# Feed-forward entries of a two-layer hybrid decoder: the clear of the last covered tile is put ahead of the step's remainder, and its values stay in that step; in the first pass the values go one step later

## The chip, the cores and the metric

The kernel runs on one core of a Trainium2 chip. Times are device microseconds (us) of one execution of the whole program. TensorE (PE) multiplies, VectorE (DVE) and ScalarE (ACT) work elementwise, GpSimd (POOL) and SyncE (SP) start most of the DMA transfers. Each engine works through its own list of instructions in order and waits on semaphores for the others.

## The reference

Two layers; each has a half-step feed-forward block, three token mixers side by side, and a second half-step feed-forward block. The change is in the feed-forward blocks alone, of which there are four in the program ("passes" below).

```python
def swiglu(h, w_in, w_out):
    gate, up = jnp.split(h @ w_in, 2, axis=-1)
    return (jax.nn.silu(gate) * up) @ w_out

for l in range(DEPTH):                                   # DEPTH = 2
    x = x + 0.5 * swiglu(rms_norm(x, ffn1_norm[l]), ffn1_w_in[l], ffn1_w_out[l])
    h = rms_norm(x, mix_norm[l]) @ w_mix_in[l]
    ...
    x = x + y @ w_mix_out[l]
    x = x + 0.5 * swiglu(rms_norm(x, ffn2_norm[l]), ffn2_w_in[l], ffn2_w_out[l])
```

x is 512 tokens by 1024 channels in float32, the hidden width is 2816.

## The kernel before, in words

Everything lies transposed: channels or hidden units on the 128 partitions, the 512 tokens along the free axis. A float32 product is made from three passes of the array: both operands are split into a rounded high part and the rest (`hi`, `lo`), and `mm3` (lines 318 to 333) issues high times high, high times low, low times high. A weight tile of 128 x 1024 is split by ACT, which copies the high part (line 801, `hl<-w`), and by DVE, which subtracts it (line 803).

The hidden units of a feed-forward block are done in two ways. The first `covered` tiles of 128 units (six in the first pass, four in the others) are plain products with the not yet normalised x, one pair of tiles at a time, while the norm and the operands of the second way are still being made. The rest goes through a Strassen-like scheme of seven products per pair of tiles, P1 to P7, each of 24 matmuls of 256 columns. These products are the *steps* of the block, numbered from 0. `halved` (line 757) runs them; in step n it issues product n, then `prepare` for the product three steps later (`LEAD = 3`: ACT's copy at once, DVE's subtraction kept as `rest`), then the elementwise work on the product's result, then whatever `self.between` holds for n, then `rest`, then the planned sums of weights (`run(n)`, line 789 among them), and last whatever `self.entry` holds for n. The order of seven products is P1, P2, P6, P5, P7, P3, P4. In the passes after the first, steps 0 to 6 and 7 to 13 are two such blocks, and step 18 is the first product of the output side, which has `m` as moving operand (line 755 makes its low part).

The results of a covered tile stay in two PSUM banks until they are *cleared*: DVE multiplies both by the reciprocal norm (`gi`, line 562, and `ui`, line 563), ACT puts `gi` through SiLU (line 274). Then the *values*: DVE multiplies `gi` by `ui` in two halves (lines 701 and 704) into the quarter tiles `hq` of the hidden activations. In passes 2 to 4 the last covered tile is cleared by the entry of step 13 and its values are the entry of step 14:

```python
        self.entry = {
            ...
            13: lambda: clear(2, 1),
            14: lambda: values(2, 1),
        }
        self.between = {4: lambda: lows["P4"]()}
```

In the first pass the loop over `halved` does both for a tile behind step 1 and for the other tile behind step 3 (lines 468 to 471). Other lines that the prediction speaks of: 904 and 888 (ACT copies the negated P1 and P6 results out of PSUM), 907 (DVE, behind P2), 916 and 919 (ACT behind P5, DVE adds the bank after P7), 922 (DVE, behind P3). P1, P6, P7 and P4 add up in one bank, so P6 can start only when line 904 has read it and P4 only when line 919 has.

Of the kernel before, what the change touches and what calls it, by code (L numbers as in the profile page):

```python
# [157 lines left out]
class Trunk:  # L158
# [292 lines left out]
    def ffn(self, w_in, w_out, next_gain, covered, begin=None, out=None):  # L451
        nc = self.nc
        tc = self.tc
        with tc.tile_pool(name=self.n("ffn"), bufs=1) as fp:
            self.tt, self.tb = "g2", 2
            if begin is not None:
                x, gain, logits = begin
            self.hq = {}
            self.entry = {}
            self.final = out is not None  # L460
            halved = self.halved(fp, w_in, w_out, covered)
            if begin is None:
                self.enter(fp, w_in, halved)
                for _ in halved:
                    pass
            else:
                finish = self.cover(fp, w_in, covered, begin, halved)
                for n, _ in enumerate(halved):

                    if n in (1, 3):  # L470
                        finish(n // 2)

            f0, nf = CHUNKS[-1]
            if next_gain is not None:
                self.begin_norm(next_gain)
            self.ntog += 1
            if out is not None:
                self.way_out(w_out, out, f0, nf)
                return
            for dg in range(2):  # L480
                banks = self.next4()

                def parts(k, kk, dg=dg):
                    r = slice((f0 + k) * P, (f0 + k + kk) * P)
                    return [w_out[r, dg * 512 : (dg + 1) * 512]]

                self.stream(
                    [(bk, slice(c, c + P), None) for bk, c in zip(banks, (0, 128, 256, 384))],
                    parts, self.last_hidden, nf,
                )  # L490
                for i in range(4):
                    j = dg * 4 + i
                    xj = self.xT[:, j, :]
                    nc.vector.scalar_tensor_tensor(
                        out=xj, in0=banks[i], scalar=0.5, in1=xj,
                        op0=ALU.mult, op1=ALU.add,
                    )
                    if next_gain is not None:
                        self.norm_part(j, fp)

    def cover(self, fp, w_in, covered, begin, then):
        nc = self.nc
        x, gain, logits = begin
        for f in range(0, covered, 2):
            banks = self.next4()

            def parts(k, kk, f=f):
                r = slice(k * P, (k + kk) * P)
                return [w_in[r, f * P : (f + 2) * P], w_in[r, FF + f * P : FF + (f + 2) * P]]

            opening = f == 0

            def norm():
                self.end_norm(
                    self.bank("pt" if self.ntog % 2 == 0 else "po"), fp,
                    self.parted_norm(fp, ("r0", "r1"), 1),
                )
                self.xparts = self.halves_of_x(fp)

                for _ in range(2):  # L520
                    next(self.xparts)


            jobs = [(bk, slice(c, c + P)) for bk, c in zip(banks, (0, 256, 128, 384))]
            if opening:
                nt = iter(["xh4", "xl4", "xh5", "xl5", "xh6", "xl6", "r2", "r3", "r4", "r5"])
                consts = self.build_consts(
                    lambda dt: fp.tile([P, T], dt, tag=next(nt), name=self.n("c"))
                )
                self.open_stream(x, gain, fp, parts, jobs, consts)  # L530
            else:
                self.stream([(*j, None) for j in jobs], parts, self.xact, KD, queued=f == 2)
            if opening:
                for _ in consts:
                    pass
                norm()
                self.lower_bounds(logits, fp.tile([P, T], F32, tag="g1", name=self.n("lb"), bufs=2))
            if f == 2:
                for _ in self.xparts:
                    pass  # L540
            if f + 4 == covered or f + 2 == covered:
                next(then)
            if opening:
                self.table(SILU)

            def finish(i, f=f, banks=banks):
                self.finish(fp, f, i, banks[2 * i], banks[2 * i + 1], f + 2 == covered)

            if f + 2 < covered:
                for i in range(2):  # L550
                    finish(i)
        return finish

    def finish(self, fp, f, i, pg, pu, keep):
        self.values(fp, f, i, *self.clear(fp, pg, pu, keep), keep)

    def clear(self, fp, pg, pu, keep):
        nc = self.nc
# [14 lines left out]
    def enter(self, fp, w_in, then):  # L573
# [68 lines left out]
        cleared = {}  # L642

        def clear(f, i):
            banks = bb if f else ba
            cleared[f, i] = self.clear(fp, banks[2 * i], banks[2 * i + 1], True)

        def values(f, i):
            self.values(fp, f, i, *cleared.pop((f, i)), True)
# [34 lines left out]
            7: lambda: values(0, 1),  # L684
            9: lambda: clear(2, 0),
            10: lambda: values(2, 0),
            13: lambda: clear(2, 1),
            14: lambda: values(2, 1),
        }
        self.between = {4: lambda: lows["P4"]()}  # L690

    def quarter(self, fp, c, a, b):
        if (c, a, b) not in self.hq:
# [327 lines left out]
    def mix(self, l, w, w_out, conv_w, out_gain, q_gain, k_gain, f_bias, next_gain):  # L1021
# [3 lines left out]
        with tc.tile_pool(name=self.n("mix"), bufs=1) as mp:  # L1025
# [181 lines left out]
            def most():  # L1207
                for dg in range(4):
# [5 lines left out]
                    for i in range(2):  # L1214
                        add(2 * dg + i, banks[i])

            beside(attend, conv(), 1, finish)
            beside(self.fox_attend(ap1, 1, half[1], qkg, {}), most())
            self.ntog = 0
# [651 lines left out]
```

## Time and profile before

| | |
|---|---|
| median of three runs | 1811.73 us (1809.85 to 1812.07) |
| the profiled execution | 1810.12 us, of which its span (first to last instruction) 1808.3 us |
| granted TensorE clock | 1.000 |
| PE busy | 1796.7 us, 99% of the span |
| DVE busy | 1453.1 us, 80% |
| ACT busy | 1000.3 us, 55% |
| POOL busy | 170.3 us, 9% |
| all DMA queues | 250.94 MB, mean 139 GB/s |

How to read it: a busy share is an average over the program, and in a profile with PE busy nearly throughout, what counts is where PE's matmuls are spaced wider than usual. The timeline lists instructions by start and duration in us; what stands in brackets at a row's end is how long the engine idled just before and what ended that. Matmuls overlap in the pipeline (each row is longer than the distance to the next one), so lost time is read from the distances between starts.

### The profile page before, as it was taken

What the parts mean: (1) busy time and instruction counts of PE and PEld (TensorE: products, weight loads), DVE (VectorE), ACT (ScalarE), POOL (GpSimd) and SP (SyncE); (2) the same over time, 40 slices, a digit from 0 to 9 for tenths busy, and PEclk for the clock granted to TensorE, in tenths of its full rate; (3) what the DMA queues carried; (4) which work ended last, traced back from release to release, by engine and by line L of the source; (5) the groups of instructions that cost most, each with busy time, mean ns of one, the idle gap of its engine ahead of it and who ended that gap; (6) DMA issues with size and microseconds to landing.
All of it is one profiled execution on the core that took longest, in us unless ns stands there. A gap on an engine that the chain in (4) does not pass through costs nothing.

```text
span 1808.3 us, 34748 instructions
## 1 busy us (share of the span) xinstructions
PE 1796.7 (99%) x14267; PEld 1681.8 (93%) x14267; DVE 1453.1 (80%) x2036; ACT 1000.3 (55%) x1437; POOL 170.3 (9%) x172
## 2 busy tenths in 40 slices
PE   9999999999999999999999999999999999999999
PEld 7899999899888899999889999998998888999997
DVE  8889787776887898879678887876868878888893
ACT  5455554464786465556445555555547855555551
POOL 0011120100000001112001111201000000020210
PEclk9999999999999999999999999999999999999999
DMA  7668783233323757868265687813333246687762
GB/s 204 181 141 187 177 180 99 71 80 83 88 77 111 218 135 164 196 161 167 82 206 132 161 190 195 167 65 83 77 90 88 72 142 184 164 156 194 157 136 94
DMA packets 243486, 250.94 MB, mean 139 GB/s; under 512 B 18520, under 2 KB 228192, under 8 KB 243328
## 3 DMA queue, kind: packets, MB, share of 16 engines
q1 hardware_dynamic: 189424, 182.38, 33.6%
q0 software_dynamic: 53600, 66.09, 23.1%
q8 instruction: 112, 1.84, 0.4%
q14 instruction: 46, 0.38, 0.1%
q10 hardware_dynamic: 304, 0.27, 0.0%
HBM read 223.98 MB, written 2.10 MB: 125 GB/s over the span
## 4 chain that ended last, share of the span: by engine, by line
PE 91%; DVE 4%; ACT 3%; issue 1%; DMA 1%; SPq 0%; ACTq 0%; DVEq 0%
PE mm L322 13%; PE mm L330 13%; PE mm L331 13%; PE sc L330 6%; PE sc L331 6%; PE sc L322 6%; PE pt L322 6%; PE pt L330 6%; PE pt L331 6%; PE po L322 4%; PE po L330 4%; PE po L331 4%; PE po L1607 1%; ACT hl L311 1%; PE pt L1649 1%
## 5 line engine op out<-in xcount | busy, mean ns | idle before, releaser
L801 ACT CAST hl<-w 128x1024 fp32r<-128x1024 f32 x322 | 336.7, 1049 | 308.7 <-PE mm L331 81.9
L803 DVE TENSOR_TENSOR hl<-w,hl 128x1024 fp32r<-128x1024 f32 x322 | 392.1, 1221 | 82.6 <-ACT hl L801 82.6
L312 DVE TENSOR_TENSOR hl<-st,hl 128x512 fp32r<-128x512 f32 (+3 forms) x192 | 162.1, 844 | 106.1 <-ACT hl L311 105.3
L311 ACT CAST hl<-st 128x512 fp32r<-128x512 f32 (+3 forms) x192 | 142.6, 743 | 170.4 <-PE po L331 64.6
L322 PE MATMUL mm<-xc,hl 128*128 128x256 f32 (+1 forms) x733 | 201.6, 276 | 0.2 <-DVE u L919 0.2
L330 PE MATMUL mm<-xc,hl 128*128 128x256 f32 x728 | 201.4, 277 | 0.0
L331 PE MATMUL mm<-xc,hl 128*128 128x256 f32 x728 | 201.1, 276 | 0.0
L322 PE MATMUL sc<-xc,hl 128*128 128x256 f32 (+1 forms) x532 | 146.0, 276 | 0.0
L330 PE MATMUL sc<-xc,hl 128*128 128x256 f32 x528 | 146.0, 276 | 0.0
L331 PE MATMUL sc<-xc,hl 128*128 128x256 f32 x528 | 145.8, 276 | 0.0
L322 PEld LDWEIGHTS mm<-xc,hl 128*128 128x128 f32 x733 | 137.4, 188 | 0.6 <-DVE u L919 0.4
L330 PEld LDWEIGHTS mm<-xc,hl 128*128 128x128 f32 x728 | 136.8, 188 | 0.0
L331 PEld LDWEIGHTS mm<-xc,hl 128*128 128x128 f32 x728 | 136.7, 188 | 0.0
L322 PE MATMUL pt<-xc,hl 128*128 128x256 f32 (+1 forms) x482 | 132.8, 276 | 0.0
L330 PE MATMUL pt<-xc,hl 128*128 128x256 f32 x480 | 132.6, 276 | 0.0
L331 PE MATMUL pt<-xc,hl 128*128 128x256 f32 x480 | 132.5, 276 | 0.0
L322 PE MATMUL mm<-x,hl 128*128 128x512 f32 x272 | 107.4, 395 | 0.0
L331 PE MATMUL mm<-x,hl 128*128 128x512 f32 x272 | 106.5, 391 | 0.0
L330 PE MATMUL mm<-x,hl 128*128 128x512 f32 x272 | 106.2, 390 | 0.0
L322 PEld LDWEIGHTS sc<-xc,hl 128*128 128x128 f32 x532 | 99.7, 188 | 0.2
L331 PEld LDWEIGHTS sc<-xc,hl 128*128 128x128 f32 x528 | 99.1, 188 | 0.0
L330 PEld LDWEIGHTS sc<-xc,hl 128*128 128x128 f32 x528 | 99.1, 188 | 0.0
(513 smaller groups left out, 5591.4 us busy)
## 6 DMA issues: line engine op xcount, KB each, us to landing
w<-in_ffn_w_in_dram SPq DMA_DIRECT2D x140, 512.0 KB
w<-in_ffn_w_out_dram SPq DMA_DIRECT2D x64, 512.0 KB
w<-in_ffn_w_out_dram POOLq DMA_DIRECT2D x56, 512.0 KB, 8.7
st<-in_w_mix_in_dram SPq DMA_DIRECT2D x88, 256.0 KB
st<-in_ffn_w_in_dram SPq DMA_DIRECT2D x70, 256.0 KB
w<-in_ffn_w_in_dram POOLq DMA_DIRECT2D x35, 512.0 KB, 8.0
w<-S POOLq DMA_DIRECT2D x35, 512.0 KB, 4.7
st<-in_ffn_w_out_dram SPq DMA_DIRECT2D x24, 512.0 KB
```

Source lines behind the costliest of these rows:

```text
L311: a = nc.scalar.copy(hi, src[:, c : c + w])
L312: b = nc.vector.tensor_sub(lo, src[:, c : c + w], hi)
L322: i = nc.tensor.matmul(acc[:, c], ah, bh[:, c], start=first and c.start == 0, stop=False, skip_group_check=True,)
L330: nc.tensor.matmul(acc, a, b, start=False, stop=False, skip_group_check=True)
L331: i = nc.tensor.matmul(acc, c, d, start=False, stop=last, skip_group_check=True)
L801: A(nc.scalar.copy(hi, src))
L803: return lambda: V(nc.vector.tensor_sub(lo, src, hi))
L1607: nc.tensor.matmul(self.ob[:, t0 + u * P : t0 + 2 * P], V[:, j, h % 4].rearrange("p a d -> p (a d)"), part[:, j, u:, :].rearrange("p i t - ...
L1649: nc.tensor.transpose(tb[:, j * P : (j + 1) * P], p[:, j * P : (j + 1) * P], self.ident)
```

## The change

In passes 2 to 4 `clear(2, 1)` moves from the entry of step 13 to `between` of step 13, that is ahead of the step's remaining subtraction, and `values(2, 1)` from the entry of step 14 to that of step 13. In the first pass the values of the second tile move from behind step 3 to behind step 4, while its clear stays. The method `finish`, which did both in one, is gone.

```diff
             else:
-                finish = self.cover(fp, w_in, covered, begin, halved)
+                clear, values = self.cover(fp, w_in, covered, begin, halved)
                 for n, _ in enumerate(halved):
-
                     if n in (1, 3):
-                        finish(n // 2)
+                        cleared = clear(n // 2)
+                    if n in (1, 4):
+                        values(n // 3, cleared)
...
-            13: lambda: clear(2, 1),
-            14: lambda: values(2, 1),
+            13: lambda: values(2, 1),
         }
-        self.between = {4: lambda: lows["P4"]()}
+        self.between = {4: lambda: lows["P4"](), 13: lambda: clear(2, 1)}
```

The lists of PE, ACT, POOL and SP keep their order; only DVE's changes, in four places. The first is in the first pass, steps 3 and 4: DVE before the change, from the clear on (`gi`, `ui`), with line 919 as `u`, line 922 as `g`, and the planned sum `S`:

```order
L562 TENSOR_TENSOR gi_925<-pt_652,inv_401 128x512
L563 TENSOR_TENSOR ui_926<-pt_653,inv_401 128x512
L701 SCALAR_TENSOR_TENSOR hq_860<-gi_925,ui_926 128x256
L704 TENSOR_TENSOR hq_862<-gi_925,ui_926 128x256
L919 TENSOR_TENSOR u_145_920<-u_145_920,mm_788 128x512
L803 TENSOR_TENSOR hl_956<-w_820,hl_956 128x1024
L789 TENSOR_TENSOR S_960<-w_782,w_820 128x1024
L922 TENSOR_TENSOR g_141_888<-g_141_888,mm_893 128x512
```

The same place with the change (its line numbers are two or three higher from here on):

```order
L565 TENSOR_TENSOR gi_925<-pt_652,inv_401 128x512
L566 TENSOR_TENSOR ui_926<-pt_653,inv_401 128x512
L921 TENSOR_TENSOR u_145_920<-u_145_920,mm_788 128x512
L805 TENSOR_TENSOR hl_954<-w_820,hl_954 128x1024
L791 TENSOR_TENSOR S_958<-w_782,w_820 128x1024
L703 SCALAR_TENSOR_TENSOR hq_860<-gi_925,ui_926 128x256
L706 TENSOR_TENSOR hq_862<-gi_925,ui_926 128x256
L924 TENSOR_TENSOR g_141_888<-g_141_888,mm_893 128x512
```

The two halves of the values have moved behind the read of the bank, the subtraction and the sum.

The second place is the end of step 13 and step 14 in the second pass; the third and fourth pass read alike but for their numbers. DVE before, from the last instruction on product 13 to the low part of `m`:

```order
L701 SCALAR_TENSOR_TENSOR hq_7397<-g_1063_7427,pt_7400 128x512
L803 TENSOR_TENSOR hl_7622<-S_7564,hl_7622 128x1024
L562 TENSOR_TENSOR gi_7629<-mm_6930,inv_6946 128x512
L563 TENSOR_TENSOR ui_7630<-po_6931,inv_6946 128x512
L803 TENSOR_TENSOR hl_7659<-w_7303,hl_7659 128x1024
L789 TENSOR_TENSOR w_7431<-S_7564,w_7532 128x1024
L704 TENSOR_TENSOR hq_7159<-gi_7629,ui_7630 128x256
L701 SCALAR_TENSOR_TENSOR hq_7161<-gi_7629,ui_7630 128x256
L907 TENSOR_TENSOR g_1086_7661<-g_1086_7661,pt_7669 128x512
L803 TENSOR_TENSOR hl_7694<-w_7566,hl_7694 128x1024
L755 TENSOR_TENSOR m_7700<-hq_7397,m_7699 128x1024
```

And with the change:

```order
L703 SCALAR_TENSOR_TENSOR hq_7397<-g_1063_7427,pt_7400 128x512
L565 TENSOR_TENSOR gi_7626<-mm_6930,inv_6946 128x512
L566 TENSOR_TENSOR ui_7627<-po_6931,inv_6946 128x512
L805 TENSOR_TENSOR hl_7622<-S_7564,hl_7622 128x1024
L706 TENSOR_TENSOR hq_7159<-gi_7626,ui_7627 128x256
L703 SCALAR_TENSOR_TENSOR hq_7161<-gi_7626,ui_7627 128x256
L805 TENSOR_TENSOR hl_7661<-w_7303,hl_7661 128x1024
L791 TENSOR_TENSOR w_7431<-S_7564,w_7532 128x1024
L909 TENSOR_TENSOR g_1086_7663<-g_1086_7663,pt_7669 128x512
L805 TENSOR_TENSOR hl_7694<-w_7566,hl_7694 128x1024
L757 TENSOR_TENSOR m_7700<-hq_7397,m_7699 128x1024
```

`gi` and `ui` stand ahead of the subtraction from `S`, the two halves of the values ahead of the next subtraction and sum; from `g` (line 907 before) on the order is as it was.

More of the change, by code (lines that the diff above doesn't have):

```diff
@@ L544, in cover, with clear, values @@
                 self.table(SILU)
-            def finish(i, f=f, banks=banks):
-                self.finish(fp, f, i, banks[2 * i], banks[2 * i + 1], f + 2 == covered)
-            if f + 2 < covered:
+            keep = f + 2 == covered
+            def clear(i, banks=banks, keep=keep):
+                return self.clear(fp, banks[2 * i], banks[2 * i + 1], keep)
+            def values(i, cleared, f=f, keep=keep):
+                self.values(fp, f, i, *cleared, keep)
+            if not keep:
                 for i in range(2):
[L551 to L555, printed above, removed]
+                    values(i, clear(i))
+        return clear, values
     def clear(self, fp, pg, pu, keep):
```

## The prediction

> **What bounds the kernel now.** First the page's busy times, then the list of waits for PE, then PE's timeline around the four places where the change moves something, and last DVE's and ACT's timelines there.
>
> ```profile
> PE 1796.7 (99%) x14267; PEld 1681.8 (93%) x14267; DVE 1453.1 (80%) x2036; ACT 1000.3 (55%) x1437; POOL 170.3 (9%) x172
> ```
>
> PE is busy for all but about 12 us of the 1808.3 us span, so the only time to be won lies in places where a matmul starts late. The list of PE's waits (engine and line <- what it waited for: us in total, times, longest) has three entries beside the moved instructions:
>
> ```profile
> PE mm L330 <- DVE m L755: 0.4, 2, 0.2
> ...
> PE mm L322 <- DVE u L919: 0.2, 1, 0.2
> PE sc L330 <- DVE m L755: 0.2, 1, 0.2
> ```
>
> That makes one wait for line 919 (first pass) and three for the low part of `m` (one for each later pass). Matmuls overlap, so these idle times understate the loss; it is read from the starts. PE's timeline in the first pass, end of step 5 and beginning of step 6 (start, duration):
>
> ```profile
> 91.95 0.28 PE L330 MATMUL mm<-xc,hl 128*128 128x256 f32 x1
> ...
> 92.40 0.28 PE L331 MATMUL mm<-xc,hl 128*128 128x256 f32 x1
> 92.88 0.38 PE L322 MATMUL mm<-xc,hl 128*128 128x256 f32 x1 [0.20 <-DVE u L919]
> 93.10 0.28 PE L330 MATMUL mm<-xc,hl 128*128 128x256 f32 x1
> ```
>
> Four regular distances (91.95 to 92.40, three rows left out in between) take 0.45 us, so one is 0.113. From 92.40 to 93.10 are two, which should take 0.225 and take 0.70: the wait costs 0.475 us, the slow distance behind it included. PE's timeline in the second pass, at the start of step 16 (P6) and of step 18 (the first product with `m`):
>
> ```profile
> 669.27 0.28 PE L331 MATMUL pt<-xc,hl 128*128 128x256 f32 x1
> 669.44 0.38 PE L322 MATMUL pt<-xc,hl 128*128 128x256 f32 x1
> 669.66 0.29 PE L330 MATMUL pt<-xc,hl 128*128 128x256 f32 x1
> 669.79 0.28 PE L331 MATMUL pt<-xc,hl 128*128 128x256 f32 x1
> ...
> 675.00 0.28 PE L322 MATMUL mm<-m,hl 128*128 128x256 f32 x1
> 675.48 0.38 PE L330 MATMUL mm<-m,hl 128*128 128x256 f32 x1 [0.20 <-DVE m L755]
> 675.70 0.28 PE L331 MATMUL mm<-m,hl 128*128 128x256 f32 x1
> ```
>
> Step 18 loses 0.70 - 0.225 = 0.475 us. Step 16 loses time too, though too little to be listed as a wait: three distances take 0.52 in place of 0.34, so 0.18. The same spot in passes 3 and 4:
>
> ```profile
> 994.52 0.28 PE L331 MATMUL po<-xc,hl 128*128 128x256 f32 x1
> 994.70 0.38 PE L322 MATMUL mm<-xc,hl 128*128 128x256 f32 x1
> 994.92 0.29 PE L330 MATMUL mm<-xc,hl 128*128 128x256 f32 x1
> ...
> 1562.96 0.28 PE L331 MATMUL pt<-xc,hl 128*128 128x256 f32 x1
> 1563.13 0.38 PE L322 MATMUL pt<-xc,hl 128*128 128x256 f32 x1
> 1563.36 0.29 PE L330 MATMUL pt<-xc,hl 128*128 128x256 f32 x1
> ```
>
> Two distances take 0.40 for 0.225: 0.175 lost in each. Their `m` waits have the same 0.2 in the list as the second pass, so I take the same 0.475.
>
> **The change part by part.** It adds and removes no instruction and no transfer; it moves instructions of DVE past others of DVE.
>
> *First pass.* DVE's timeline there, from the second multiplication of the clear on:
>
> ```profile
> 90.62 0.68 DVE L563 TENSOR_TENSOR ui<-pt,inv 128x512 f32<-128x512 f32 x1
> 91.47 0.43 DVE L701 SCALAR_TENSOR_TENSOR hq<-gi,ui 128x256 f32<-128x256 f32 x1 [0.17 <-ACT gi L274]
> ...
> 92.15 0.68 DVE L919 TENSOR_TENSOR u<-u,mm 128x512 f32<-128x512 f32 x1
> 92.74 1.22 DVE L803 TENSOR_TENSOR hl<-w,hl 128x1024 fp32r<-128x1024 f32 x1
> 93.88 1.22 DVE L789 TENSOR_TENSOR S<-w,w 128x1024 f32<-128x1024 f32 x1
> 95.02 0.68 DVE L922 TENSOR_TENSOR g<-g,mm 128x512 f32<-128x512 f32 x1
> ```
>
> Line 919 reads the bank that step 6 (P4) is waiting for. Its own product, P7, ended a whole product (24 x 0.113 = 2.7 us) before 92.4, so it could have run at 90; it stood behind two halves of values, which also waited 0.17 for SiLU. Rows without a wait follow each other after 0.60 (512 columns), 0.34 (256) and 1.14 (1024). With the values out of the way line 919 starts at 90.62 + 0.60 = 91.22 in place of 92.15 and frees the bank at about 91.95, ahead of the 92.51 at which P4 is due. The wait goes: -0.475 us. What is late next: the values now run behind the sum, and line 922 comes behind them. At worst (sum no earlier than before) it starts at 95.02 + 0.67 = 95.69, 0.67 late; at best the 0.93 gained ahead is kept and it starts 0.26 early. Behind it stands the subtraction for product 8, which starts by 96.29 and is usable 1.28 later (as from the start of the low part of `m`, 674.20 in a row below, to its matmul at 675.48), at 97.6; product 8 starts at 92.51 + 2 x 2.71 = 97.9 and wants the low part with its third matmul at 98.2. A margin of 0.6 remains, so this costs nothing; POOL's next accumulating transfer, which waits for this subtraction, starts up to 0.7 us later, and no weight transfer stands in PE's list. Bounds for the part: -0.475 and, should the margin fail by all of the 0.67, +0.2; I take -0.475.
>
> *Passes 2 to 4.* DVE's timeline in the second pass as it was:
>
> ```profile
> 665.47 1.22 DVE L803 TENSOR_TENSOR hl<-S,hl 128x1024 fp32r<-128x1024 f32 x1
> 666.61 0.68 DVE L562 TENSOR_TENSOR gi<-mm,inv 128x512 f32<-128x512 f32 x1
> 667.21 0.68 DVE L563 TENSOR_TENSOR ui<-po,inv 128x512 f32<-128x512 f32 x1
> 668.93 1.23 DVE L803 TENSOR_TENSOR hl<-w,hl 128x1024 fp32r<-128x1024 f32 x1 [1.04 <-ACT hl L801]
> ...
> 671.88 0.68 DVE L907 TENSOR_TENSOR g<-g,pt 128x512 f32<-128x512 f32 x1
> 672.47 1.22 DVE L803 TENSOR_TENSOR hl<-w,hl 128x1024 fp32r<-128x1024 f32 x1
> 674.20 1.23 DVE L755 TENSOR_TENSOR m<-hq,m 128x1024 fp32r<-128x1024 f32 x1 [0.51 <-ACT m L755]
> ```
>
> and ACT's:
>
> ```profile
> 667.32 0.63 ACT L274 ACTIVATE gi<-gi 128x512 f32<-128x512 f32 x1 [2.08 <-DVE gi L562]
> 667.86 1.03 ACT L801 CAST hl<-w 128x1024 fp32r<-128x1024 f32 x1
> 668.80 0.59 ACT L904 ACTIVATE g<-pt 128x512 f32<-128x512 f32 x1
> ...
> 672.59 0.63 ACT L274 ACTIVATE g<-g 128x512 f32<-128x512 f32 x1 [1.91 <-DVE g L907]
> 673.13 1.04 ACT L755 CAST m<-hq 128x1024 fp32r<-128x1024 f32 x1
> ```
>
> The two engines hand one chain to and fro: clear on DVE, SiLU, copy and line 904 on ACT (PE's step 16 waits for 904), and DVE stands still for 1.04 us until the copy is done. Then sum, values, 907, again SiLU, and only behind it ACT's copy of `m`, DVE's low part, step 18.
>
> With the change: `gi` 665.47, `ui` 666.07, subtraction from `S` 666.67, values 667.81 and 668.15. SiLU follows its `gi` by 0.71 as it does now, at 666.18, and ends around 666.8, a microsecond ahead of the values. ACT's copy behind it also waits for the end of product 14 (24 distances before 669.38, so 666.67); I give the signal half a microsecond and let it start at 667.17 in place of 667.86. Line 904 follows by 0.94 at 668.11 and ends by 668.7, ahead of the 669.38 at which P6 is due. So 0.18 (0.175 in passes 3, 4) goes. DVE's next subtraction starts at 668.48 (its copy, started 1.07 ahead in the rows, is ready at 668.24: no standstill), the sum at 669.62, line 907 at 670.76 in place of 671.88. SiLU 671.47, copy of `m` 0.54 later at 672.01, low part 1.07 behind that (674.20 - 673.13) at 673.08, done at 674.36. Step 18 now starts at 675.00 - 0.18 and wants it with the second matmul at 674.95: a margin of 0.59. The `m` wait goes too, -0.475. What is late next is the subtraction from `S`, 1.2 us later and ready at 667.95; product 16 wants it with its third matmul at 669.61, a margin of 1.66. No transfer waits for that one; those that wait for the others start earlier.
>
> All this leans on the distances of 0.60 and 1.14, each 0.08 shorter than the row's own duration. The Trainium skill, in "VectorE: DVE Perf Modes", section "The DRAIN you can't avoid", says that the next Vector operation doesn't start until the pipe is empty, while adding that one that isn't held starts earlier. Taken strictly, that would put the seven instructions from `gi` to 907 0.08 later each, 0.56 in all, and the margin of 0.59 would be gone; the rows here start before their predecessor's end, so the trace sides with the exception.
>
> Sum: 0.475 + (0.18 + 0.475) + 2 x (0.175 + 0.475) = 2.43 us. Against the profiled execution (1810.12, which is the span plus 1.8) that gives 1807.7; the median of the three runs lies 1.6 above the profiled one, and from it the time is 1811.73 - 2.4 = 1809.3.
>
> **The rivals.**
>
> *Only the small waits go* (chance 0.13). The `m` wait stays in passes 2 to 4, because line 907 or the copy of `m` comes less early than worked out; it takes 0.59 us of error in a chain of eight instructions. For it speaks that the chain changes engine four times; against it that every hop is taken from a row. Gain 0.475 + 0.18 + 2 x 0.175 = 1.0: 1810.7.
>
> *The gain doesn't reach the end* (0.07): PE arrives 2.4 us earlier in all, and the mixers' chains through DVE and ACT, which cause PE's longest waits, take it back: 1811.7. Against it: these chains start from PE's products and would move along.
>
> *More than the sum* (0.14): the runs shown and the profiled one lie in two pairs, at 1810 and at 1812. Where the median of the changed kernel falls into the lower pair, the sum gives 1809.85 - 2.4 = 1807.4, 4.3 below the median of before.
>
> *Slower* (0.06): the clear, now in front of the subtraction from `S`, doesn't find its inputs or buffers free and holds DVE. There are two buffers each of `gi` and `ui`, shared with the blocks' own `g` and `u`. If it had to wait for the end of product 15 (669.4, say 669.6 with the signal), the subtraction would be ready at 669.6 + 1.2 + 1.28 = 672.1, 2.5 us behind P6's 669.61; with the slow distance 2.6, three times 7.8, less the first pass's gain: 1811.7 + 7.3 = 1819.0. It decides from a wait of 1.66 us on. Against it: the buffers' last readers are DVE's own instructions just ahead, and the banks have been full since long before step 13.
>
> **How the numbers follow.** The forecast has the remaining 0.60: 1809.3. About 0.2% of this time, 3.6 us, is what a measurement of this kernel can tell from no change. The three runs spread by 2.2, so a forecast of -2.4 passes -3.6 in about one case in six of its 0.60, 0.10; with the case of more than the sum that makes 0.24 faster. Slower is its rival's 0.06; 0.70 remain within 0.2%. The range leaves out the slower rival and the tails: from 1807.0 (just under the lower pair less 2.4) to 1811.9 (no gain).
>
> **What would show it.** In the changed kernel's PE list the entries for line 919 and line 755 are gone; the distances at the starts of steps 16 and 18 are 0.11; DVE's 1.04 standstill ahead of its subtraction in step 14 is gone, and line 907 there starts 1.4 us behind the end of product 15 (670.76 against 669.38) where it was 2.5. A row naming `hl` with `S` as PE's releaser at step 16, or DVE waiting for SiLU at the values, would make it wrong.

## The result and the profile after

| | before | changed |
|---|---|---|
| median | 1811.4 us (21 runs, 1809.85 to 1812.47) | 1808.03 us (21 runs, 1806.67 to 1810.77) |
| ratio | | 0.9983, 95% interval 0.9977 to 0.9989 |
| span of the profiled execution | 1808.3 us | 1806.7 us |

The changed kernel is faster by 0.17%, 2.0 to 4.2 us by the interval; the sum on record, 2.43 us, is a ratio of 0.9987 and lies inside. The time came in at 1808.0 where 1809.3 was forecast. The forecast that the change stays within 0.2% (3.6 us) held narrowly: the medians differ by 3.4 us.

PE's list of waits of the changed kernel, whole (engine and line <- what it waited for: us in total, times, longest; all line numbers here but 322 are two higher than before):

```profile
PE pt L1651 <- DVE T L1473: 2.6, 2, 1.5
PE mm L1765 <- DVE z L1752: 1.2, 1, 1.2
PE po L1609 <- ACT PH L1653: 0.8, 2, 0.4
PE sc L1586 <- DVE nm L1591: 0.7, 2, 0.4
PE pt L1651 <- DVE KB L1571: 0.4, 2, 0.2
PE mm L322 <- DVE zf L1125: 0.4, 1, 0.4
PE sc L1586 <- DVE fo L1623: 0.2, 1, 0.2
PE po L1609 <- DVE PL L1654: 0.2, 1, 0.2
```

The line that read the bank (919, now 921) and the one that makes the low part of `m` (755, now 757) are gone from it. PE's timeline at the three kinds of place, first step 6 of the first pass, then steps 16 and 18 of the second:

```profile
92.72 0.28 PE L331 MATMUL mm<-xc,hl 128*128 128x256 f32 x1
92.83 0.28 PE L322 MATMUL mm<-xc,hl 128*128 128x256 f32 x1
...
669.47 0.28 PE L331 MATMUL pt<-xc,hl 128*128 128x256 f32 x1
669.59 0.28 PE L322 MATMUL pt<-xc,hl 128*128 128x256 f32 x1
669.70 0.28 PE L330 MATMUL pt<-xc,hl 128*128 128x256 f32 x1
...
675.03 0.28 PE L322 MATMUL mm<-m,hl 128*128 128x256 f32 x1
675.14 0.28 PE L330 MATMUL mm<-m,hl 128*128 128x256 f32 x1
```

Each distance is 0.11 now, where it was 0.48, 0.17 and 0.22, and 0.48. DVE's timeline in the second pass, from `gi` to the low part of `m`, and under it ACT's:

```profile
665.67 0.69 DVE L565 TENSOR_TENSOR gi<-mm,inv 128x512 f32<-128x512 f32 x1
666.27 0.69 DVE L566 TENSOR_TENSOR ui<-po,inv 128x512 f32<-128x512 f32 x1
666.87 1.22 DVE L805 TENSOR_TENSOR hl<-S,hl 128x1024 fp32r<-128x1024 f32 x1
...
668.67 1.23 DVE L805 TENSOR_TENSOR hl<-w,hl 128x1024 fp32r<-128x1024 f32 x1
669.81 1.23 DVE L791 TENSOR_TENSOR w<-S,w 128x1024 f32<-128x1024 f32 x1
670.95 0.69 DVE L909 TENSOR_TENSOR g<-g,pt 128x512 f32<-128x512 f32 x1
...
673.27 1.22 DVE L757 TENSOR_TENSOR m<-hq,m 128x1024 fp32r<-128x1024 f32 x1 [0.51 <-ACT m L757]
```

```profile
666.39 0.63 ACT L274 ACTIVATE gi<-gi 128x512 f32<-128x512 f32 x1 [0.94 <-DVE gi L565]
667.11 1.05 ACT L803 CAST hl<-w 128x1024 fp32r<-128x1024 f32 x1
668.06 0.59 ACT L906 ACTIVATE g<-pt 128x512 f32<-128x512 f32 x1
```

This execution runs 0.20 us behind that of before at this place (665.67 against 665.47). Less that, the rows are the worked ones: the subtraction from `S` 666.67, line 907 (now 909) 670.75 where 670.76 was forecast, the low part of `m` 673.07 for 673.08. DVE's 1.04 us of standstill ahead of its subtraction in step 14 is filled. The low part is there at 673.27 + 1.28 = 674.55 and the matmul starts at 675.14: the margin is 0.59, as in the prediction.

The spans of these two executions differ by only 1.6 us. Matmul by matmul, the seven places give 2.5 us, and a slow stretch of before right behind one of them gives another 0.5 (last section). Against that stand losses at places the change doesn't touch: the first pass's norm (line 440) starts 0.3 later, the first layer's mixers take 0.4 longer, and slow stretches in the second layer's mixers cost 0.6; smaller differences both ways make up the rest. Such things differ from one execution to the next. Line 440's matmuls (min, median, max in ns; first and last start) in two of the runs below, the one with only the values early and the one with both again:

```profile
L440 PE MATMUL po<-sh,ones_mean x2: 494/499/504, 31.1 to 32.4; 128*128 128x512 f32 x2
```

```profile
L440 PE MATMUL po<-sh,ones_mean x2: 500/500/501, 32.9 to 34.3; 128*128 128x512 f32 x2
```

This opening lies ahead of every moved instruction, and it alone moves by 1.8 us from one execution to another. So a difference of 2 us is read from the distances at its places, and the timing can only be asked whether it agrees.

### The profile page after: what moved, and what is told of

It reads as the page before. It is cut to its first block, busy times and chain, and to the rows that moved or that the text cites. A ratio compares the mean times of both kernels' runs of the same rounds, so it can differ in the third digit from the quotient of the medians.

```text
span 1806.7 us, 34748 instructions
## 1 busy us (share of the span) xinstructions
PE 1795.8 (99%) x14267; PEld 1681.3 (93%) x14267; DVE 1453.4 (80%) x2036; ACT 1000.7 (55%) x1437; POOL 170.4 (9%) x172
## 4 chain that ended last, share of the span: by engine, by line
PE 92%; DVE 3%; ACT 3%; issue 1%; DMA 1%; SPq 0%; ACTq 0%; DVEq 0%
PE mm L322 13%; PE mm L330 13%; PE mm L331 13%; PE sc L330 6%; PE sc L331 6%; PE sc L322 6%; PE pt L322 6%; PE pt L330 6%; PE pt L331 6%; PE po L330 4%; PE po L322 4%; PE po L331 4%; ACT hl L311 1%; PE po L1609 1%; PE pt L1651 1%
```

## The experiments

Theory: each lost stretch of PE has its own chain on DVE and ACT, and the time saved is the sum of those stretches. Rival: the measured 3.4 us come from elsewhere. The runs with the first pass alone, with passes 2 to 4 alone, with both again and with six repeats were timed on one chip against 27 runs of before (median 1810.45), the other four on another chip against 33 (1810.93). The diffs of the first two are cut from the diff against the kernel before, the later ones are against the changed kernel.

**The first pass alone.** Of the diff only the first hunk; the entries of steps 13 and 14 stay.

```diff
                     if n in (1, 3):
-                        finish(n // 2)
+                        cleared = clear(n // 2)
+                    if n in (1, 4):
+                        values(n // 3, cleared)
```

> Only the first pass is changed (values of its second tile one step later); passes 2 to 4 are as before. Chain theory (each lost stretch of PE has its own cause on DVE and ACT, and the time is the sum of the stretches): in the profile the wait of 0.475 us at the start of step 6 of the first pass is gone, the three losses of 0.175 to 0.18 at step 16 and the three of 0.475 at step 18 are all still there; time about 0.5 us below before, which a measurement of this kernel can hardly tell from none. Rival (the 3.4 us measured come from somewhere else than these waits): no telling by place; the first pass alone would bring a share other than 0.475 of 2.43.

Measured: 1809.35 us, ratio 0.9995 (0.9987 to 1.0004), an interval that holds the expected 0.5 us as well as no change. PE's list of waits has no entry for the bank any more and still has the three for `m`:

```profile
PE mm L330 <- DVE m L758: 0.4, 2, 0.2
...
PE sc L330 <- DVE m L758: 0.2, 1, 0.2
```

The distances at step 16 are as wide as before in all three passes (0.17 and 0.22).

**Passes 2 to 4 alone.** The second hunk; in the first pass both still behind step 3.

```diff
-            13: lambda: clear(2, 1),
-            14: lambda: values(2, 1),
+            13: lambda: values(2, 1),
...
-        self.between = {4: lambda: lows["P4"]()}
+        self.between = {4: lambda: lows["P4"](), 13: lambda: clear(2, 1)}
```

> Only passes 2 to 4 are changed (clear ahead of the remainder of step 13, values in the same step); the first pass is as before. Chain theory: the six losses in passes 2 to 4 are gone, 0.18 + 2 x 0.175 + 3 x 0.475 = 1.95 us, the wait for the bank in the first pass (0.475) stays; time 2.0 us below before. Rival (the gain lies elsewhere): the time stays within 1 us of before, or falls by all 3.4.

Measured: 1807.99 us, ratio 0.9988 (0.9980 to 0.9997), 2.2 us. The six losses are gone and the one in the first pass stands, in PE's timeline:

```profile
92.40 0.28 PE L331 MATMUL mm<-xc,hl 128*128 128x256 f32 x1
92.88 0.38 PE L322 MATMUL mm<-xc,hl 128*128 128x256 f32 x1 [0.20 <-DVE u L921]
```

The two parts are independent of each other: each removes its own losses and no others.

**Both again.** No edit to the changed kernel.

> The changed kernel once more, beside the others on one chip. Chain theory: 2.4 us below before (ratio 0.9987), all seven losses gone. Rival (more than these waits goes): 3.4 us below again (ratio 0.9981), and the profile shows a further place, met in each profile of the changed kernel, where PE is ahead.

Measured: 1807.85 us, ratio 0.9987 (0.9979 to 0.9996): 2.35 us on this chip, the sum. All seven losses are gone again. Against the profile of before, both profiles of the changed kernel are ahead at one further place, by 0.5 us behind step 18 of the third pass. There the profile of before has a slow stretch (last section); the run with the first pass alone, which keeps the wait at that step, hasn't. So this gain belongs to that one execution of before.

**Only the clear ahead.** The values of passes 2 to 4 go back one step.

```diff
-            13: lambda: values(2, 1),
+            14: lambda: values(2, 1),
```

> The changed kernel with one half of its edit in passes 2 to 4 undone: the clear stays ahead of the remainder of step 13, the values go back to the entry of step 14. Chain theory: SiLU, ACT's copy and line 904 are as early as in the changed kernel, so the loss at step 16 is gone; DVE's subtraction of step 14 now waits 0.2 for its copy instead of doing the values meanwhile, line 907 comes 0.2 later than in the changed kernel and the low part of m keeps 0.4 of its margin, so the loss at step 18 is gone as well: 2.4 us below before. Rival (it is the early values that free the chain): step 18 keeps its 0.475 in each pass, 1.0 below before.

Measured: 1806.96 us, ratio 0.9981 (0.9972 to 0.9989), 2.0 to 5.1 us for the expected 2.4. Both losses are gone in all three passes. DVE's timeline in the second pass, line 907 (here 909) and the low part of `m`, and PE's at step 18:

```profile
670.05 0.68 DVE L909 TENSOR_TENSOR g<-g,pt 128x512 f32<-128x512 f32 x1
...
672.38 1.23 DVE L757 TENSOR_TENSOR m<-hq,m 128x1024 fp32r<-128x1024 f32 x1 [0.51 <-ACT m L757]
```

```profile
673.94 0.28 PE L322 MATMUL mm<-m,hl 128*128 128x256 f32 x1
674.05 0.28 PE L330 MATMUL mm<-m,hl 128*128 128x256 f32 x1
```

The low part is usable at 672.38 + 1.28 = 673.66, 0.39 ahead of 674.05, where 0.4 was expected. The clear ahead suffices; the early values only widen the margin.

**Only the values early.** The clear goes back behind the remainder, the values follow it at once.

```diff
-            13: lambda: values(2, 1),
+            13: lambda: (clear(2, 1), values(2, 1)),
...
-        self.between = {4: lambda: lows["P4"](), 13: lambda: clear(2, 1)}
+        self.between = {4: lambda: lows["P4"]()}
```

> The changed kernel with the other half undone in passes 2 to 4: the clear goes back behind the remainder of step 13, the values follow it at once in the entry of that step. Chain theory: SiLU and with it line 904 are as late as before, so step 16 keeps its 0.18; DVE uses its standstill of 1.04 us for the values, line 907 comes 0.67 earlier than before (671.21 on the clock of the prediction), the low part of m is usable at 674.8 where step 18 wants it at 675.11, so that loss goes with a margin of 0.3: 0.475 + 3 x 0.475 = 1.9 below before. Rival (only a clear ahead of the remainder frees the chain): both losses stay, 0.5 below before.

Measured: 1807.85 us, ratio 0.9982 (0.9973 to 0.9991), whose interval holds the expected 1.9 us (0.9990). ACT's line 904 (here 906) is late and step 16 keeps its loss, while step 18 starts without a wait:

```profile
667.32 0.59 ACT L906 ACTIVATE g<-pt 128x512 f32<-128x512 f32 x1
```

```profile
667.79 0.28 PE L331 MATMUL pt<-xc,hl 128*128 128x256 f32 x1
667.96 0.38 PE L322 MATMUL pt<-xc,hl 128*128 128x256 f32 x1
668.18 0.29 PE L330 MATMUL pt<-xc,hl 128*128 128x256 f32 x1
...
673.52 0.28 PE L322 MATMUL mm<-m,hl 128*128 128x256 f32 x1
673.63 0.28 PE L330 MATMUL mm<-m,hl 128*128 128x256 f32 x1
```

Together with the run before this one, this tells the two losses apart: line 904 is early only if the clear is, while either half of the edit brings the low part of `m` in time.

**The margins, by weight on DVE.** In three kernels the second multiplication of the last clear is repeated in passes 2 to 4 (k = 6, 1 and 2; the same values are written each time).

```diff
-        V(nc.vector.tensor_mul(ui, pu, self.inv))
+        for _ in range(1 + extra):
+            V(nc.vector.tensor_mul(ui, pu, self.inv))
```

Six repeats:

> The changed kernel, with the second multiplication of the clear of step 13 done seven times over in passes 2 to 4 (the same result written each time): 6 x 0.60 = 3.6 us more on DVE in front of the subtraction from S. Chain theory, by the starts of the prediction: that subtraction is ready at 671.55 where product 16 wants it at 669.61, a wait of 1.9 at step 16; line 907 starts at 674.36, the copy of m 1.25 later, its low part is usable at 677.96 where step 18, itself 2 us late, wants it at 676.98, a wait of 1.0; with the slow distance behind each 3.1 us in each of three passes, so 9.4 above the changed kernel and 7 above before. Rival (DVE, 80% busy, is no bound and has slack for it): within 1 us of the changed kernel.

Measured: 1820.38 us, ratio 1.0059 (1.0046 to 1.0073), 12.5 us above the changed kernel on this chip (1807.85) where 9.4 was expected. PE's list of waits names the subtraction from `S`, which the prediction's slower rival priced, and `m`:

```profile
PE pt L331 <- DVE hl L808: 5.0, 2, 2.5
...
PE mm L331 <- DVE hl L808: 2.5, 1, 2.5
PE mm L330 <- DVE m L760: 1.6, 2, 0.8
```

Most of the miss is in the weight. DVE's timeline:

```profile
665.08 5.03 DVE L567 TENSOR_TENSOR ui<-po,inv 128x512 f32<-128x512 f32 x7
670.02 1.21 DVE L808 TENSOR_TENSOR hl<-S,hl 128x1024 fp32r<-128x1024 f32 x1
```

Seven take 4.94 us; less 0.60 for the last, six repeats weigh 4.34, so 0.72 each and not 0.60: a repeat starts after its predecessor's end and not 0.08 ahead of it. In the trace each repeat waits for a semaphore that DVE itself raises with the instruction ahead; the first of the seven has no such wait. With 4.34 the same chain gives 2.68 and 0.95 us of waiting and 0.11 behind each, 3.85 a pass; the distances in passes 2 and 4 show 3.84. The third pass lost 4.4, as the clock fell behind its step 16 (last section).

One repeat, with 0.72:

> The changed kernel with the second multiplication of the clear of step 13 done twice in passes 2 to 4. A repeat took 0.72 us in the kernel with six of them. Chain theory: the subtraction from S keeps 0.9 of its margin of 1.66 and step 16 starts on time; the low part of m loses its margin of 0.59 and comes 0.13 late, with the slow distance behind it 0.24 us lost at step 18 of each of the three passes, 0.7 in all above the changed kernel. Rival (slack on DVE hides so little): none lost.

Measured: 1808.22 us, ratio 0.9986 (0.9977 to 0.9995). Step 16 starts on time in each pass. Step 18's start in PE's timeline, second pass:

```profile
672.77 0.39 PE L330 MATMUL mm<-m,hl 128*128 128x256 f32 x1
672.99 0.28 PE L331 MATMUL mm<-m,hl 128*128 128x256 f32 x1
```

The distance to the matmul ahead of 672.77 is 0.248 and the next is 0.22, so 0.24 us is lost, as expected. Two repeats:

> The same with two repeats, 1.44 us more on DVE. Chain theory: step 16 still starts on time (margin 1.66 - 1.44 = 0.2), step 18 waits 0.85 for the low part of m and loses 0.96 with the slow distance, 2.9 us in three passes above the changed kernel, 0.5 above before. Rival (the subtraction from S is the tighter one): a loss at step 16, none at step 18.

Measured: 1810.25 us, ratio 0.9997 (0.9988 to 1.0006).

```profile
673.97 0.28 PE L322 MATMUL mm<-m,hl 128*128 128x256 f32 x1
674.93 0.38 PE L330 MATMUL mm<-m,hl 128*128 128x256 f32 x1 [0.69 <-DVE m L760]
675.16 0.28 PE L331 MATMUL mm<-m,hl 128*128 128x256 f32 x1
```

0.96 and 0.23 for 0.225: 0.96 lost, and again nothing at step 16. So the 0.59 of margin is real: one repeat overshoots it by 0.13, two by 0.85, and the timing is no longer told from that of before. The two runs differ by 2.0 us, where three times 0.96 less 0.24 make 2.2.

## Why the prediction was right

- *PE's distances are the price list.* The seven losses went, each by its size, and the parts alone removed their own. The sum of 2.43 was measured as 2.35 in the run on one chip with the parts and as 2.0 to 4.2 in the first comparison. The forecast of the time lay 1.3 us too high: 0.3 of it is its base, the median of three runs (1811.73) where 21 give 1811.4, the rest is what the comparison shows beyond the sum.
- *First pass.* Line 919 follows `ui` by 0.60 (90.94 to 91.54). Line 922 came out between its two bounds: it starts 4.74 behind `ui` (95.68) where it was 4.40 (95.02 against 90.62), so it moved 0.34 back, neither 0.67 back nor 0.26 ahead. Of the 0.93 gained ahead of it only 0.33 was kept, since DVE now stands 0.51 for ACT's copy before its subtraction. The margin that covered it held.
- *Passes 2 to 4.* Every start was within 0.02 us of its working but for ACT's copy, to which I gave half a microsecond of signal, and line 904 behind it; the copy came 0.26 earlier than that, at 666.91 on the prediction's clock. That hid nothing and cost nothing. One sum was 0.02 off: 674.82 and a distance of 0.113 make 674.93, not 674.95.
- *The Trainium skill's rule.* What "VectorE: DVE Perf Modes", section "The DRAIN you can't avoid", says of the pipe that must empty would have eaten the margin. These rows start 0.08 ahead of their predecessor's end, as in the trace of before, so the exception that the section adds is the case here. Only the repeats, which the program makes wait for DVE's own semaphore, start 0.72 apart.
- *The rivals.* "Only the small waits go" fell by the margin, which the weights measured. "The gain doesn't reach the end" fell by the timings. "Slower" didn't arise: `gi` starts 0.60 behind the row ahead of it (665.07 to 665.67), so the clear waited for no buffer and no bank. Only the margin that priced it was tried: step 16 loses time under a weight of 4.34 and not under 1.44, which brackets its point of 1.66. The price itself left out step 18, which loses another 1.06 under six repeats. "More than the sum" stays open. Its ground, two levels of before at 1810 and 1812, was chance, for the 21 runs fill the span from 1809.85 to 1812.47. By the ratios the four runs on the second chip gain 0.8 to 1.4 us more than their sums, those with the parts and with both -0.1 to 0.4 more, each within its interval. The four share their runs of before, and one and two repeats differ among themselves by what the distances say (2.0 for 2.2); that points to the comparison rather than to one of the edits, but isn't shown. Of what lies beyond the sum only 0.5 us has a place in a profile, the slow stretch in that of before; whether other executions of before have it is not known.

## What to carry to other kernels

Where one engine is busy 99% of the time, read the distances between its starts: three of the seven losses here were in no list of waits. The starts behind a small reordering can then be worked out to hundredths of a microsecond by walking the hand-over chain instruction by instruction, with the gap between rows and not the row's duration; write down the margin left behind, since it is what the next edit will use up. Put the head of a chain that another engine waits for ahead of work with margin, and put what follows into a standstill of its own engine rather than behind it.

## What the runs showed of the hardware

Under six repeats PE lost about 2.7 us at step 16 in each of three passes (2.5 us idle by the trace), and in the third pass, the second of the three cases, the granted clock then fell to one half. A table of stretches of that pass (length; busy us of PE, PEld, DVE, ACT and POOL with counts; granted clock; DMA share; GB/s), and PE's rows as the clock drops:

```profile
994.00:1000.50 6.50, 3.98 (x35) 3.78 (x34) 6.29 (x11) 2.89 (x4) 0.34 (x1) 1.00 0.91 144
1000.50:1003.90 3.40, 3.40 (x19) 3.40 (x18) 3.40 (x4) 0.61 (x2) 0.00 (x0) 0.50 0.35 101
```

```profile
1000.62 0.42 PE L331 MATMUL mm<-xc,hl 128*128 128x256 f32 x1
1000.84 0.42 PE L322 MATMUL mm<-xc,hl 128*128 128x256 f32 x1
```

Matmuls stand 0.21 apart for 3.4 us. The other two standstills, as long, left the clock at 1.00. The Trainium skill ("TensorE: Matmul & The Clock Gate", section "What's actually happening") describes a clock gate that judges PE's activity in windows of about 3.4 us that run freely and goes to the half rate after at least one idle window. The length of the slow stretch agrees, and windows that run freely would fit that only one of three such cases shows it. But PE stood still for only 2.5 us ahead of it, less than such a window, so the idle window isn't borne out here.

PE also has a slower pace at full clock. In the profile of before it begins right behind the late start of step 18 in the third pass:

```profile
1000.73 0.38 PE L330 MATMUL sc<-m,hl 128*128 128x256 f32 x1 [0.20 <-DVE m L755]
1000.95 0.28 PE L331 MATMUL sc<-m,hl 128*128 128x256 f32 x1
```

The same stretch of time in before and in the changed kernel, in the columns of the table above:

```profile
1001.00:1014.80 13.80, 13.80 (x119) 13.80 (x119) 10.96 (x12) 6.97 (x8) 0.00 (x0) 1.00 0.58 180
```

```profile
1001.00:1014.80 13.80, 13.80 (x124) 13.80 (x123) 10.94 (x13) 6.43 (x8) 0.00 (x0) 1.00 0.49 155
```

From 1000.95 on, 118 distances are 0.1178 each, where the regular one is 0.1133; that is 0.53 us, more than the wait itself cost. In the mixers the same stretches of some 45 and 95 matmuls ran at the one pace in some profiles and at the other in others. In all ten profiles each such stretch of 20 or more begins right behind a wide distance (0.17 to 0.22 us). Most late matmuls aren't followed by one, though: of the 28 at steps 6, 16 and 18 in these profiles this is the only one with a long stretch. The others have at most four slower distances behind them, if the one ahead of the clock's fall is left aside. What decides between the two paces wasn't tried.
